# Moving the adaLN gate's pieces, one weight sum and the DRAM sums in a hybrid-head block

## The chip, the cores and the metric

The kernel runs on one core of a Trainium2 chip, as one program. The metric is the device time of one execution in microseconds (us), the median of several runs. PE is TensorE (matmuls), PEld its weight loads, DVE is VectorE, ACT is ScalarE, POOL is GpSimd, SP is SyncE, which only issues DMAs here. ACT and POOL issue DMAs too.

## The reference

One layer with 512 tokens, width 2048, all in float32. `c` is one row of 2048, `w_ada` is 2048 x 12288.

```
mod = silu(c) @ w_ada + b_ada;   sh1, sc1, gt1, sh2, sc2, gt2 = split(mod, 6)
h   = rms_norm(x, g_mix) * (1 + sc1) + sh1
... h @ w_in -> a recurrent group and an attention group -> mix
x   = x + gt1 * (mix @ w_out)
h2  = rms_norm(x, g_ffn) * (1 + sc2) + sh2
gate, up = split(h2 @ w_up, 2)                 # w_up 2048 x 11264
x   = x + gt2 * ((silu(gate) * up) @ w_down)   # w_down 5632 x 2048
```

The change touches how `gt2` is computed and spread, and how the weights of the last two products are summed.

## The kernel before

Every matmul is done in three parts: an operand is split into a high part, rounded to the fast float format by ACT (`hi`, L248), and a rest, taken by DVE (`lo`, L249); PE adds hi*hi, hi*lo and lo*hi. `wsplit` does this for weights; each call leaves its two instructions in `tail_hi` and `tail_lo`, after which other work can be ordered (`tc.issue_after`).

The order of each engine's instructions is made when the program is built, by priority and by which buffers are free; `tc.high_priority(offset=...)` moves a piece of work ahead. A tile that finds no free buffer of its tag waits for the release of an older one. Each engine then runs its list in that order.

The work goes through stages: input projection, heads and recurrence, output projection (`wo`), then two ordinary groups of the up projection (`up0`, `up1`, by `fm_group`, steps 0 to 15 each), then ten upper blocks (`NBLK`), then the down projection in four phases.

*The upper blocks* multiply quarter blocks in Strassen's manner, with seven products in place of eight. In block `b` the products go in the order 4, 5, 1, 7, 6, 2, 3, numbered i = 0 to 6 in the schedule; each has eight steps j, and a hook `(i, j)` is work placed behind step j of the i-th product. Four weight units of 2 MB each (U_A, U_C, U_B, U_D) are loaded by SP into six tiles of 1 MB, two with the tag `raw` and four with `raw2`; `IN_RAW` says which units go to `raw`. DVE adds units to one another (`sum_unit`, L1144, two instructions a sum) before products 5, 7, 6 and 3. Products leave PSUM as pages `us` and `uu` of the tag `c`. This tag has 16 pages, 8 of which hold the second operand through all blocks. Finished blocks are transposed and written to DRAM as `td` (`back`, `keep_act`) in the next block.

*gt2* is a matrix-vector product done on DVE: the class `Gt2` takes 64 pieces of 128 x 512 weights, times the matching quarter of silu(c) (`gt2_r_None`, read from DRAM with broadcast), six or seven in each block (`GT2_N`). Loads are issued by ACT (L192), pieces run on DVE (L200) at the hooks `GT2_STEPS`. At most four pages are live, and each piece asks for the next load. `gt2_sum` adds the partial sums to a 128 x 16 tile. `gt2_spread`, called at the fourth step of the first down phase, writes this tile to DRAM transposed, so that each float lands by itself (L1313, four DMAs of POOL), and reads it back as four broadcast tiles `gt2b` (L1317), which are needed at the end of the third phase.

*DRAM sums.* The down projection is also done in Strassen's manner, and needs sums of its weight quarters. They are made in DRAM, for eleven parts q: `sums24(q, 0)` copies two quarters (SP, L1080 and L1081), `sums24(q, 1)` and `(q, 2)` add a quarter each by accumulating DMAs of POOL (L1073), and `(q, 3)` adds one sum to the other. They hang on the half products of the upper blocks (`SUMS_AT`, `SUMS_PER`).

*The first down phase* computes products 4 and 5 in turn, 22 steps. Product 4's weights come into `raw` (two tiles), product 5's into `raw2`; product 5 needs the sum of both (L1281), which frees product 4's tile for the next load (L1249).

Of the kernel before, what the change touches and what calls it, by code (L numbers as in the profile page):

```python
# [31 lines left out]
SH1, SC1, GT1, SH2, SC2, GT2 = range(6)  # L32
# [24 lines left out]
KEEP = (2, 8, 2)  # L57
GT2_STEPS = ((4, 4), (4, 6), (5, 0), (5, 2), (5, 4), (5, 6), (6, 0))
GT2_N = (6, 6, 6, 6, 6, 6, 7, 7, 7, 7)
SUMS_AT, SUMS_PER = 24, 10  # L60
BU_PART = (0, 5, 10, 16)
# [9 lines left out]
def block_kernel(ctx, tc, xT, crow, adaT, vecs, bfr, w1, wyr, wqkv0, wqkv, wgate, wout, wup0, wups, wdn, outT):  # L71
# [105 lines left out]
    class Gt2:  # L177
        def __init__(self, pieces):
            self.items, self.live, self.pages = [], 0, {}
            for n, (r, i) in enumerate(pieces):  # L180
                if n == 0 or pieces[n - 1][0] != r:
                    self.items.append((r, None))
                self.items.append((r, i))
            self.pieces = list(pieces)

        def loads(self):
            while self.items and self.live < 4:
                r, i = self.items.pop(0)
                cs = slice(r * S, (r + 1) * S)
                t = page(f"gt2_{r}_{i}", "d")  # L190
                with tc.issue_after(tail_hi[-1]):
                    nc.scalar.dma_start(out=t, in_=c_d[:, cs].broadcast_to([P, S]) if i is None else adaT[GT2 * KT + i, :, cs])  # L192
                self.pages[r, i] = t
                self.live += 1

        def piece(self):
            r, i = self.pieces.pop(0)
            t, c = self.pages.pop((r, i)), self.pages[r, None]
            with tc.issue_after(tail_lo[-1]), tc.high_priority(offset=AHEAD):
                nc.vector.scalar_tensor_tensor(out=t, in0=t, scalar=1.0, in1=c, op0=ALU.mult, op1=ALU.mult,  # L200
                                               accum_out=gt2_acc[:, r, i:i + 1])
            self.live -= 2 if not self.pieces or self.pieces[0][0] != r else 1
            self.loads()
# [12 lines left out]

    tail_lo, tail_hi = [], []

    def ada_some(n, ahead=True):
# [35 lines left out]
    def stream(src, kts, width, name, raw_hook=None, ahead=AHEAD):  # L255
        for q in range(len(kts) // 4):
            with tc.high_priority(offset=ahead):
                raw = wp.tile([P, 2048], F32, tag="raw", name=f"{name}r{q}", bufs=RAW)
                nc.sync.dma_start(out=raw[:, :4 * width], in_=src[kts[q * 4] // 4])
            if raw_hook:  # L260
# [814 lines left out]
    def sums24(q, n):  # L1075
        if n == 0:
            with tc.issue_after(up_loads[-1]):
                for i in range(2):
# [18 lines left out]
    for gi in range(STD):  # L1097
        hk = {}
        if gi == 0:
# [3 lines left out]
            add(hk, R1STEP[1], lambda: r1.append(r1_spread()))  # L1103
            add(hk, X_STEPS[3], lambda: x1_by_tokens(3))
        for j in range(4):
            add(hk, T_STEPS[gi][j], lambda j=j + 4 * gi: make_t(j))
# [11 lines left out]
    U_A, U_C, U_B, U_D = range(4)  # L1118
    IN_RAW = (2, 4, 9, 11)
    ORDER = (4, 5, 1, 7, 6, 2, 3)  # L1120
# [4 lines left out]
    def load_unit(b, u):  # L1125
        tiles = []
        mine = len(loads) % 12 in IN_RAW
        loads.append((b, u))
# [17 lines left out]
    def prod_weights(p, b, un):  # L1146
        with tc.high_priority(offset=AHEAD):
# [11 lines left out]
            elif p == 2:  # L1159
                un[U_D] = load_unit(b, U_D)  # L1160
            else:
                sum_unit(un[U_D], un[U_A])
            src = un[{4: U_A, 5: U_A, 1: U_B, 7: U_C, 6: U_A, 2: U_D, 3: U_D}[p]]
        for q in range(4):
# [17 lines left out]
    for b in range(NBLK):  # L1182
        un, keep_ = {}, {}
        gt2 = Gt2(gt2_left[:GT2_N[b]])
        del gt2_left[:GT2_N[b]]
        add(hk, (4, 1), gt2.loads)
        for _, at in zip(range(GT2_N[b]), GT2_STEPS):
            add(hk, at, gt2.piece)
        for i, p in enumerate(ORDER):
# [3 lines left out]
            for j, hi, lo in prod_weights(p, b, un):  # L1193
# [8 lines left out]
                if j % 4 == 3:  # L1202
                    n = halves - SUMS_AT
                    halves += 1
                    if 0 <= n < SUMS_PER * NQ and n % 2 == 0 and n % SUMS_PER < 8:
                        sums24(n // SUMS_PER, n % SUMS_PER // 2)
            if b + i == 0:
# [102 lines left out]
    def gt2_spread():  # L1310
        gd = drp.tile([KT, P], F32, name="gt2d")
        for a in range(4):
            nc.gpsimd.dma_start(out=gd[4 * a:4 * a + 4].rearrange("k p -> p k"), in_=mods[GT2][:, 4 * a:4 * a + 4])  # L1313
        gv = gd.rearrange("(a k) p -> a k p", k=4)
# [150 lines left out]
```

## Time and profile before

| | us |
|---|---|
| median of 3 runs | 2070.2 (2069.98 to 2072.98) |
| the profiled execution | 2063.58, its span 2061.9 |
| PE, DVE, ACT busy | 2017.4, 1676.1, 983.7 |
| upper blocks | 816.8 to 1614.2 |
| first down phase | 1614.2 to 1757.0 |

The profile is one execution, so its stretches add up to the span, not to the median. Times in rows of a chain or a timeline are from the span's start. A row of waits reads: engine and line that waited, what ended the wait, total, number of waits, longest. A name such as `up_2p` leaves out the block's number: the PSUM tile of product 2; `up_3l` is the lo part of the fourth quarter of a product's weights, and `dq_3r` a weight tile of part 3 of the down projection, of any product.

### The profile page before, as it was taken

What the parts mean: (1) busy time and instruction counts of PE and PEld (TensorE: products, weight loads), DVE (VectorE), ACT (ScalarE), POOL (GpSimd) and SP (SyncE); (2) the same over time, 40 slices, a digit from 0 to 9 for tenths busy, and PEclk for the clock granted to TensorE, in tenths of its full rate; (3) what the DMA queues carried; (4) which work ended last, traced back from release to release, by engine and by line L of the source; (5) the groups of instructions that cost most, each with busy time, mean ns of one, the idle gap of its engine ahead of it and who ended that gap; (6) DMA issues with size and microseconds to landing.
All of it is one profiled execution on the core that took longest, in us unless ns stands there. A gap on an engine that the chain in (4) does not pass through costs nothing.

```text
span 2061.9 us, 25612 instructions
## 1 busy us (share of the span) xinstructions
PE 2017.4 (98%) x9329; PEld 1690.5 (82%) x9329; DVE 1676.1 (81%) x2300; ACT 983.7 (48%) x1361; POOL 108.5 (5%) x142
## 2 busy tenths in 40 slices
PE   9999999999999999999999999999999889999998
PEld 7889998888888888887888788878878768888887
DVE  8999768987687779797797797897887857777786
ACT  4433447764522366444444444544444435545443
POOL 0000001111000000001000000010000010000000
PEclk9999999999999999999999999999999999999999
DMA  9989766767588762449989977997985787777793
GB/s 350 355 299 334 247 212 221 231 217 249 191 277 315 267 225 89 136 135 284 252 203 299 267 193 242 259 255 235 251 237 169 193 221 240 260 252 254 266 327 120
DMA packets 173779, 496.33 MB, mean 241 GB/s; under 512 B 18546, under 2 KB 41234, under 8 KB 169555
## 3 DMA queue, kind: packets, MB, share of 16 engines
q1 hardware_dynamic: 151252, 434.80, 62.2%
q0 software_dynamic: 11168, 39.60, 10.9%
q10 hardware_dynamic: 11232, 20.30, 3.2%
q8 instruction: 73, 1.20, 0.2%
q14 instruction: 54, 0.44, 0.1%
HBM read 458.93 MB, written 93.36 MB: 268 GB/s over the span
## 4 chain that ended last, share of the span: by engine, by line
PE 61%; DVE 21%; DMA 8%; issue 8%; ACT 1%; POOL 1%; SPq 0%; ACTq 0%; DVEq 0%; POOLq 0%
PE up_5p L253 5%; PE up_1p L253 5%; PE w1p L253 4%; DVE uw L1144 4%; PE up_7p L253 3%; PE dn6p L253 3%; PE dn3p L253 3%; PE dn2p L253 3%; PE dn1p L253 3%; PE dn7p L253 3%; PE yr1p L253 2%; PE yr0p L253 2%; PE up0p L253 2%; PE wo2p L253 2%; PE wo3p L253 2%
## 5 line engine op out<-in xcount | busy, mean ns | idle before, releaser
L1144 DVE TENSOR_TENSOR uw<-uw,uw 128x2048 f32<-128x2048 f32 x80 | 182.7, 2294 | 0.0
L248 ACT ACTIVATE up_0h<-uw 128x1024 fp32r<-128x1024 f32 x70 | 74.3, 1062 | 157.3 <-DVE uw L1144 65.6
L162 DVE SCALAR_TENSOR_TENSOR ada<-ada,c_b 128x1024 f32<-128x1024 f32 x96 | 116.3, 1222 | 31.0 <-DMA ada<-in_adaT 30.5
L248 ACT ACTIVATE up_1h<-uw 128x1024 fp32r<-128x1024 f32 x70 | 74.2, 1059 | 95.2 <-PE up_5p L253 16.5
L249 DVE TENSOR_TENSOR up_2l<-uw,up_2h 128x1024 fp32r<-128x1024 f32 x70 | 85.9, 1226 | 38.9 <-ACT up_2h L248 38.6
L249 DVE TENSOR_TENSOR up_1l<-uw,up_1h 128x1024 fp32r<-128x1024 f32 x70 | 85.8, 1225 | 32.2 <-ACT up_1h L248 32.2
L248 ACT ACTIVATE up_3h<-uw 128x1024 fp32r<-128x1024 f32 x70 | 74.3, 1061 | 67.5 <-PE up_2p L253 13.9
L248 ACT ACTIVATE up_2h<-uw 128x1024 fp32r<-128x1024 f32 x70 | 74.1, 1059 | 58.0 <-PE up_3p L253 13.2
L249 DVE TENSOR_TENSOR up_0l<-uw,up_0h 128x1024 fp32r<-128x1024 f32 x70 | 85.8, 1225 | 17.8 <-ACT up_0h L248 17.7
L249 DVE TENSOR_TENSOR up_3l<-uw,up_3h 128x1024 fp32r<-128x1024 f32 x70 | 85.7, 1225 | 14.9 <-ACT up_3h L248 14.2
L1073 POOL DMA_DIRECT2D s2d<-in_wdn x44 | 36.4, 833 | 632.3 <-DMA s2d<-in_wdn 632.3
L200 DVE SCALAR_TENSOR_TENSOR gt<-gt,gt_None 128x512 f32<-128x512 f32 x64 | 44.1, 688 | 18.1 <-DMA gt<-in_adaT 12.5
L253 PE MATMUL w1p<-hpl,w1h 128*128 128x512 f32 x128 | 49.8, 389 | 0.0
L253 PE MATMUL w1p<-hph,w1l 128*128 128x512 f32 x128 | 49.8, 389 | 0.0
L172 DVE SCALAR_TENSOR_TENSOR ada<-ada,c_b 128x1024 f32<-128x1024 f32 x32 | 39.1, 1221 | 4.1 <-DMA ada<-in_adaT 4.1
L253 PE MATMUL w1p<-hph,w1h 128*128 128x512 f32 x128 | 42.4, 391 | 0.0
L172 DVE SCALAR_TENSOR_TENSOR adf<-adf,c_b 128x1024 f32<-128x1024 f32 x32 | 39.1, 1222 | 0.4 <-DMA adf<-in_adaT 0.4
L606 ACT ACTIVATE bt<-bt,nm 128x128 f32<-128x128 f32 (+3 forms) x32 | 18.0, 561 | 40.1 <-DVE nm L604 39.8
L685 DVE SCALAR_TENSOR_TENSOR ba<-bw,sh,ba 128x512 f32<-128x512 f32 x45 | 32.8, 750 | 3.3 <-DMA bw<-in_w 2.2
L951 DVE SCALAR_TENSOR_TENSOR bu_acc<-bu,mod,bu_acc 128x512 f32<-128x512 f32 x30 | 22.5, 750 | 13.3 <-DMA bu<-in_wup 12.8
L253 PEld LDWEIGHTS w1p<-hph,w1h 128*128 128x128 f32 x128 | 23.9, 188 | 5.5 <-ACT hph L413 0.7
L413 ACT ACTIVATE hph<-x,A 128x512 fp32r<-128x512 f32 x16 | 11.6, 725 | 35.0 <-DVE A L410 35.0
(2291 smaller groups left out, 6651.5 us busy)
## 6 DMA issues: line engine op xcount, KB each, us to landing
uw<-in_wups SPq DMA_DIRECT2D x160, 512.0 KB, 7.1
ada<-in_adaT SPq DMA_DIRECT2D x128, 512.0 KB, 5.6
s2d<-in_wdn POOLq DMA_DIRECT2D x44, 512.0 KB, 7.9
adf<-in_adaT SPq DMA_DIRECT2D x32, 512.0 KB, 6.3
gt<-in_adaT ACTq DMA_DIRECT2D x64, 256.0 KB, 6.6
s2d<-in_wdn SPq DMA_DIRECT2D x22, 512.0 KB, 10.4
s4d<-in_wdn SPq DMA_DIRECT2D x22, 512.0 KB, 11.1
s4d<-s2d POOLq DMA_DIRECT2D x22, 512.0 KB, 9.4
```

The lines of the kernel that those rows point to most:

```text
L162: nc.vector.scalar_tensor_tensor(out=t, in0=t, scalar=1.0, in1=cs, op0=ALU.mult, op1=ALU.mult, accum_out=ac)
L172: nc.vector.scalar_tensor_tensor(out=t, in0=t, scalar=1.0, in1=c_b[:, cs], op0=ALU.mult, op1=ALU.mult, accum_out=ada_acc[j][:, hf, i:i + 1])
L200: nc.vector.scalar_tensor_tensor(out=t, in0=t, scalar=1.0, in1=c, op0=ALU.mult, op1=ALU.mult, accum_out=gt2_acc[:, r, i:i + 1])
L248: tail_hi.append(nc.scalar.activation(R(hi[:, :n]), raw_ap, AF.Copy).ins)
L249: tail_lo.append(nc.vector.tensor_sub(R(lo[:, :n]), raw_ap, hi[:, :n]).ins)
L253: nc.tensor.matmul(ps, lhsT=R(l), rhs=R(r), start=start, stop=stop)
L413: nc.scalar.activation(R(h), xt, AF.Copy, scale=a)
L606: nc.scalar.activation(p[:, :n], p[:, :n], AF.Exp, scale=-1.0, bias=nm, accum_out=sm)
L685: nc.vector.scalar_tensor_tensor(out=ba[j], in0=src, scalar=s1, in1=ba[j], op0=ALU.mult, op1=ALU.add)
L951: nc.vector.scalar_tensor_tensor(out=a, in0=src, scalar=s2, in1=a, op0=ALU.mult, op1=ALU.add)
L1073: nc.gpsimd.dma_start(out=out[:, cs], in_=src[:, cs], accum_op=ALU.add)
L1144: nc.vector.tensor_add(d_, d_, s_)
```

## The change

- `Gt2`: the loads begin at hook (3, 3) in place of (4, 1); six pages may be live in place of four, the first two of a block taken from the tag `c`; the pieces run at (4, 1), (4, 2), (4, 3), (4, 5), (4, 7), (5, 1), (5, 3).
- The sum for product 3 goes into U_A and product 3 reads U_A; before it went into U_D. With it, the units that use `raw` follow a period of 8, not 12.
- `gt2_spread` writes gt2 to DRAM by one DMA of SP in place of four of POOL.
- The DRAM sums of part 0 are made in the groups `up0` (steps 1, 8, 15) and `up1` (step 6); those of the other ten parts begin at half product 4, one every 13 halves.

```diff
-GT2_STEPS = ((4, 4), (4, 6), (5, 0), (5, 2), (5, 4), (5, 6), (6, 0))
+GT2_STEPS = ((4, 1), (4, 2), (4, 3), (4, 5), (4, 7), (5, 1), (5, 3))
-SUMS_AT, SUMS_PER = 24, 10
+SUMS_AT, SUMS_PER = 4, 13
+SUMS_STEPS = ((1, 8, 15), (6,))
...
-            self.items, self.live, self.pages = [], 0, {}
+            self.items, self.live, self.pages, self.tags = [], 0, {}, ["c", "c"]
...
-            while self.items and self.live < 4:
+            while self.items and self.live < 6:
...
-                t = page(f"gt2_{r}_{i}", "d")
+                t = page(f"gt2_{r}_{i}", self.tags.pop(0) if self.tags else "d")
...
-            self.live -= 2 if not self.pieces or self.pieces[0][0] != r else 1
+            self.live -= 1 if self.pieces and self.pieces[0][0] == r else 2
...
-            with tc.issue_after(up_loads[-1]):
+            with tc.issue_after((up_loads or stream_loads)[-1]):
...
+        for i, n in enumerate(SUMS_STEPS[gi]):
+            add(hk, n, lambda i=i + 3 * gi: sums24(0, i))
...
-    IN_RAW = (2, 4, 9, 11)
+    IN_RAW = (2, 4)
...
-        mine = len(loads) % 12 in IN_RAW
+        mine = len(loads) % 8 in IN_RAW
...
-                sum_unit(un[U_D], un[U_A])
-            src = un[{4: U_A, 5: U_A, 1: U_B, 7: U_C, 6: U_A, 2: U_D, 3: U_D}[p]]
+                sum_unit(un[U_A], un[U_D])
+            src = un[{4: U_A, 5: U_A, 1: U_B, 7: U_C, 6: U_A, 2: U_D, 3: U_A}[p]]
...
-        add(hk, (4, 1), gt2.loads)
+        add(hk, (3, 3), gt2.loads)
...
-                    if 0 <= n < SUMS_PER * NQ and n % 2 == 0 and n % SUMS_PER < 8:
-                        sums24(n // SUMS_PER, n % SUMS_PER // 2)
+                    if 0 <= n < SUMS_PER * (NQ - 1) and n % SUMS_PER % 3 == 0 and n % SUMS_PER < 12:
+                        sums24(1 + n // SUMS_PER, n % SUMS_PER // 3)
...
-        for a in range(4):
-            nc.gpsimd.dma_start(out=gd[4 * a:4 * a + 4].rearrange("k p -> p k"), in_=mods[GT2][:, 4 * a:4 * a + 4])
+        nc.sync.dma_start(out=gd.rearrange("k p -> p k"), in_=mods[GT2])
```

More of the change, by code (lines that the diff above doesn't have):

```diff
@@ L217, in block_kernel @@
     tail_lo, tail_hi = [], []
+    stream_loads = []
     def ada_some(n, ahead=True):
@@ L258, in stream @@
                 raw = wp.tile([P, 2048], F32, tag="raw", name=f"{name}r{q}", bufs=RAW)
-                nc.sync.dma_start(out=raw[:, :4 * width], in_=src[kts[q * 4] // 4])
+                ld = nc.sync.dma_start(out=raw[:, :4 * width], in_=src[kts[q * 4] // 4])
+                stream_loads.append(ld.ins)
             if raw_hook:
```

## The prediction

> **What bounds the kernel now.** I read the page's busy table first, then the time by stretches, then who waited for whom, then the chain that ended last in the two places where PE loses time.
>
> ```profile
> span 2061.9 us, 25612 instructions
> PE 2017.4 (98%) x9329; PEld 1690.5 (82%) x9329; DVE 1676.1 (81%) x2300; ACT 983.7 (48%) x1361; POOL 108.5 (5%) x142
> ```
>
> PE is busy 2017.4 of 2061.9 us. None of the edits touches a matmul, so all that can be won is PE's idle time. The stretches below are cut where PE starts each of the ten upper blocks; the last two rows are the first and the second phase of the down projection. The columns are length, busy time of PE, PEld, DVE, ACT, POOL, granted clock, DMA share and GB/s.
>
> ```profile
> core 0: us, PE busy (x) PEld busy (x) DVE busy (x) ACT busy (x) POOL busy (x), PEclk, DMA share, GB/s
> 816.80:893.00 76.20, 76.20 (x338) 63.09 (x337) 64.80 (x73) 36.62 (x41) 0.00 (x0) 1.00 0.46 146
> 893.00:973.60 80.60, 78.96 (x353) 64.32 (x352) 67.03 (x74) 37.72 (x44) 4.58 (x6) 1.00 0.67 190
> 973.60:1052.70 79.10, 78.64 (x354) 64.60 (x352) 68.01 (x76) 37.72 (x44) 5.53 (x7) 1.00 0.86 249
> 1052.70:1131.20 78.50, 78.37 (x354) 64.61 (x353) 67.78 (x76) 37.97 (x44) 9.84 (x12) 1.00 0.99 262
> 1131.20:1210.80 79.60, 79.05 (x354) 64.44 (x353) 67.43 (x76) 37.85 (x44) 4.91 (x6) 1.00 0.86 246
> 1210.80:1289.30 78.50, 78.37 (x354) 64.61 (x353) 67.75 (x77) 37.95 (x44) 4.94 (x6) 1.00 0.81 224
> 1289.30:1371.20 81.90, 78.89 (x353) 64.42 (x352) 67.79 (x76) 37.70 (x44) 9.85 (x12) 1.00 0.99 257
> 1371.20:1450.40 79.20, 78.56 (x354) 64.59 (x354) 68.19 (x78) 38.11 (x44) 4.92 (x6) 1.00 0.85 249
> 1450.40:1532.80 82.40, 79.06 (x354) 64.44 (x352) 68.30 (x78) 37.86 (x44) 9.82 (x12) 1.00 0.99 256
> 1532.80:1614.20 81.40, 79.28 (x354) 64.44 (x352) 68.10 (x78) 38.71 (x46) 0.00 (x0) 1.00 0.56 181
> 1614.20:1757.00 142.80, 128.39 (x545) 101.25 (x544) 98.71 (x96) 63.30 (x79) 10.57 (x16) 0.96 0.79 217
> 1757.00:1876.70 119.70, 119.70 (x529) 99.06 (x528) 90.49 (x78) 59.30 (x72) 0.00 (x0) 1.00 0.72 245
> ```
>
> A block without stalls takes 78.5 us (two of them do). The nine blocks behind the first exceed it by 2.1 + 0.6 + 0 + 1.1 + 0 + 3.4 + 0.7 + 3.9 + 2.9 = 14.7 us. The two down phases have the same 22 steps. The second runs without a gap in 119.7 us; the first takes 142.8, of which 1.8 are the last block's 16 transposes (an estimate, from the 0.11 us between their starts), so it loses 21.3 us. These two sums, 36 us, are the stake.
>
> ```profile
> PE up_2p L253 <- DVE up_3l L249: 4.2, 3, 1.7
> PE up_3p L253 <- DVE up_1l L249: 3.5, 4, 1.2
> ...
> DVE gt L200 <- DMA gt<-in_adaT: 12.5, 11, 2.1
> ...
> ACT up_0h L248 <- DVE uw L1144: 65.6, 17, 5.7
> ...
> 1330.37 8.28 DMA gt<-in_adaT
> ...
> 1341.15 10.94 DMA gt<-in_adaT
> ...
> 1352.88 2.20 DVE uw L1144
> ...
> 827.85 10.88 PE up_5p L253 x48
> ```
>
> In the blocks, PE waits in products 2 and 3 for DVE's lo splits. DVE runs in order, and a gt2 piece (L200) that stands before a split waits for its load: 12.5 us in 11 waits. The chain of the dear block at 1289 to 1371 goes through two such loads, then the sum of U_D (L1144), which stands between splits of products 2 and 3. A product is 10.88 us, a step 1.36.
>
> ```profile
> PE dn4p L253 <- ACT dq_3w0h L248: 8.3, 1, 8.3
> ...
> 1643.96 0.61 PE L253 MATMUL dn5p<-dq_1w1h,dq_1tl 128*128 128x512 f32 x2
> ...
> 1625.39 4.36 DMA dq_2r<-in_wdn
> ...
> 1637.20 16.54 DMA dq_3r<-in_wdn
> ...
> 1659.37 9.45 DMA dq_4r<-in_wdn
> ...
> 1674.45 8.62 DMA dq_5r<-in_wdn
> ...
> 1688.71 6.49 DMA dq_6r<-in_wdn
> ...
> L1313 POOL DMA_DIRECT2D gt2d<-mod x4: 757/766/852, 1626.5 to 1665.4; - x4
> DMA to landing us min/median/max: 11.1/13.0/13.5
> ```
>
> In the first down phase the chain is load after load: product 4's next weight tile has only two buffers and can be fetched only once the sum for product 5 has read the old one. Such a load takes 4.36 us where nothing disturbs it. The four behind it take 12.2, 5.1, 4.3 and 2.1 us more, 23.7 in all, which covers the 21.3 lost. They are slow exactly while the four writes of gt2 to DRAM are under way (L1313, first 1626.5, last 1665.4 plus 13). What the DMA engines moved in the stretches between the reading of such a write and its landing, and in the undisturbed rest of the phase:
>
> ```profile
> 1631.00:1639.00 8.00, 7.75 (x34) 5.94 (x33) 7.13 (x8) 3.59 (x4) 1.23 (x2) 1.00 1.11 87
> ...
> 1648.00:1654.00 6.00, 1.10 (x2) 0.50 (x2) 1.12 (x1) 1.21 (x2) 0.00 (x0) 0.54 0.90 124
> 1658.00:1666.00 8.00, 8.00 (x35) 6.54 (x35) 4.02 (x4) 2.64 (x3) 0.61 (x1) 0.96 0.63 78
> ...
> 1672.00:1679.00 7.00, 5.34 (x23) 3.79 (x22) 4.41 (x3) 2.00 (x2) 0.65 (x2) 1.00 0.90 94
> 1708.00:1757.00 49.00, 49.00 (x217) 40.56 (x217) 38.29 (x34) 26.10 (x34) 0.00 (x0) 1.00 0.73 247
> ```
>
> 8 KB in single floats holds up all queues for 8 + 6 + 8 + 7 = 29 us, at 78 to 124 GB/s against the 247 that the phase takes when it runs freely. The 8.3 us wait also drops the granted clock to 0.54 behind it.
>
> **The change, part by part.**
>
> *gt2 pieces and their pages.* The same 64 pieces, six or seven a block, and the same loads. Before, the shared row of c and three pieces are asked for at step (4,1), and the first piece comes three steps, 4.1 us, later; each further load waits on ACT for a page that a piece frees, and its piece follows six steps, 8.2 us, behind. After, the row and five pieces go out at (3,3), six steps ahead of the first piece at (4,1); the sixth and seventh are asked for at (4,1) and (4,2) and used eight and nine steps, 10.9 and 12.2 us, later.
>
> ```profile
> DMA to landing us min/median/max: 2.9/6.6/12.4
> ```
>
> That row is the landing time of the gt loads. The median is covered everywhere; only the slowest (blocks where the DRAM copies of s2d and s4d go out just then) will still make DVE wait a little. ACT holds one or two late loads a block instead of three or four, so its hi splits behind them are freer. A price on the other side: 1.5 MB now leave at (3,3) beside the next block's weights, and the first two pages come from the pool that U2's tile needs at the end of product 6; that tile then waits for the last piece, at (5,1) or (5,3). DVE reaches these positions about when product 6 ends, so I cost it at nothing, at most 1 us in blocks of seven pieces.
>
> *The sum for product 3 goes into U_A.* Same two DVE instructions of 2.2 us. Into U_D each half had to wait until product 2's splits had read it; into U_A it needs only product 6's splits done and U_D landed, both earlier. So the sum leaves the narrow place between product 2 and product 3. U_D is free before U_A now, the order is swapped, and the buffer choice (period 8 instead of 12) fits that; loads have a product or more of lead, cost nothing.
>
> *DRAM sums.* Same bytes, one of eleven sums moved into the two groups ahead of the blocks, the others every 13 halves instead of 10. The DMA share of the first block is 0.46 and of others up to 0.99, so the work goes where there is room; the SP queue ahead of the blocks carries 2 MB more among stream loads. I cost it at nothing; if its cover there is gone, one weight load of 4.36 us comes late once.
>
> Of the blocks' 14.7 us, 12.3 lie in the four with over 2 us each, all of this kind. Bounds: 13 gained; 3 lost if the earlier burst only moves the waits. What is late next is DVE itself, 68 of 78.5 us busy. I take 8 gained, nearer the upper end, because the two waits are removed where the chain has them.
>
> *gt2 to DRAM by SP.* Four POOL instructions of 0.77 us go, one SP instruction comes. POOL no longer holds the last td writes. On SP the write stands among the weight loads. Its input is ready before POOL's first write at 1626.5, and SP's next load goes out later:
>
> ```profile
> 1629.06 0.80 SPq L1249 DMA_DIRECT2D dq_4r<-in_wdn  x2
> ```
>
> So SP waits for nothing new; but in its queue the loads now stand behind 2048 single floats. No row shows such a write from SP. Bounds: as short as one of the four (8 us), or as long as all (29 us). With a start at 1627.5 and 3 us for what queued up, the one load exposed, issued at 1637.2, lands at 1659.5 in the long case: it takes 22.3 us, 17.9 too long, 5.8 less than the 23.7 of before. In the short case it is undisturbed, and nearly all 21.3 are won. Twice the 29 is rival 4 below. I take the middle, 18.5 us: lands at 1649, 7.4 too long, 16.3 less than before; scaled by 21.3/23.7 about 14 us won. Reason: the elements are the same, but the set-up and the final receipt of each of the four (a landing of 13 us against 6 to 8 us of slow traffic) are paid once.
>
> **Sum.** -8 - 14 = -22 us. The profiled execution took 2063.6 us (span 2061.9 and 1.7 around it); the median of the runs shown, 2070.2, is 6.6 above it, and I take the difference over unchanged: 2070.2 - 22 = 2048.
>
> **The rivals.**
> 1. *The price of the write is kept.* Nothing is saved but the repeats: -5.8 there, -8 in the blocks, 2056. For it: the packets of all queues stand still together, as if one place took the floats one by one. The Trainium skill says the same: by "DMA: Bandwidth & Descriptors", Rules for kernel authors, a strided last dimension makes one descriptor for each element, and by its section "Issuing engines are not separate DMA queues" another issuing engine saves only issue time. The stretches above, slow for all queues at once, agree with the second.
> 2. *The write from SP is nearly free.* -20 there, -10 in the blocks: 2040. For it: a 512-float write took 13 us, far more than its bytes; against: no row of SP with single floats.
> 3. *The burst at (3,3) collides.* Blocks gain 0 to 1, the write 14: 2056. For it: landings up to 12.4 us; against: 4 us more lead.
> 4. *Slower: each float costs twice as much from SP,* since each goes as a packet of its own and SP's own loads stand behind it. 58 us from 1627.5, plus 3: the load takes 51 us, 47 too long, 23 more than before; with -8 that is +15, 2085. It decides from a blockade of 43 us on, where the load is 32 us late: 1.5 times the 29 seen.
> 5. *Nothing happens:* the stalls reappear behind DVE, the write costs 35 us; 2066 to 2074.
>
> **How the numbers follow.** Forecast 0.42, rivals 0.17, 0.13, 0.08, 0.12, 0.08. 0.2% (4 us) is about what a measurement of this kernel can tell from no change. Faster: 0.42 + 0.16 + 0.13 + 0.07 = 0.78; slower: 0.12; the same: 0.10. Range 2038 to 2074: from rival 2 up to rival 5; rival 4 and a tip of rival 2 stay out. The forecast's own range is 2042 to 2054.
>
> **What would show it.** Blocks of 78.5 to 79.5 us, DVE's waits for gt under 5 us, no PE wait in product 3: the first two edits right. One gt2d row from SP with a landing near 20 us, one slow dq load, first down phase near 128 us: the write right. A landing over 45 us, or a PE wait over 25 us at the fourth step, would make the forecast wrong; so would blocks that stay at 81 us, with ACT or DVE waiting at product 6.

## The result, and the profile after

The changed kernel takes 2061.6 us (median of 5 runs, 2059.2 to 2064.6) against 2070.0 (2067.7 to 2073.0) for the kernel before on the same chip: a ratio of 0.996, 95% interval 0.9945 to 0.9974. It is faster by 8.4 us, where 22 were forecast; the time lies inside the range given.

The page of the changed kernel: PE has the same work, and its span is only 2.2 us shorter than that of before. The profiled execution of before (2063.6) lay under all five runs of this comparison, so the two profiles show 2.2 of the 8.4 us. They serve to say where time came and went; how much the change is worth is read from the medians.

```profile
span 2059.7 us, 25583 instructions
PE 2017.1 (98%) x9329; PEld 1695.0 (82%) x9329; DVE 1674.8 (81%) x2300; ACT 987.2 (48%) x1361; POOL 107.0 (5%) x138
```

The stretches of the changed kernel, cut where PE starts an upper block, with the columns of the prediction's table (length, busy PE, PEld, DVE, ACT, POOL, granted clock, DMA share, GB/s). The last row is the first down phase.

```profile
828.75:904.91 76.16, 76.16 (x337) 63.08 (x336) 66.57 (x75) 36.64 (x41) 4.11 (x5) 1.00 0.73 204
...
983.08:1061.23 78.15, 78.15 (x353) 64.59 (x352) 67.47 (x76) 38.30 (x44) 4.95 (x6) 1.00 0.80 225
...
1139.38:1219.22 79.84, 78.92 (x354) 64.35 (x352) 67.38 (x75) 38.07 (x44) 9.07 (x11) 1.00 0.94 251
1219.22:1303.24 84.02, 79.80 (x353) 65.52 (x352) 67.81 (x76) 38.20 (x44) 4.95 (x6) 0.98 0.74 218
1303.24:1381.44 78.20, 78.20 (x353) 64.50 (x352) 68.07 (x77) 38.41 (x44) 4.92 (x6) 1.00 0.74 217
1381.44:1466.73 85.29, 81.24 (x353) 65.97 (x352) 68.39 (x78) 38.20 (x44) 4.94 (x6) 0.96 0.74 221
1466.73:1546.52 79.79, 78.72 (x353) 64.43 (x352) 68.05 (x77) 38.10 (x44) 4.92 (x6) 1.00 0.81 225
...
1626.20:1755.26 129.06, 124.00 (x546) 101.67 (x545) 98.09 (x92) 65.64 (x82) 7.46 (x12) 0.99 0.75 255
```

Three things happened. The first block starts at 828.75 instead of 816.80: 12.0 us lost ahead of the blocks, a place to which the prediction gave no stall. The first down phase became 13.6 us shorter, as forecast. The ten blocks together did not change (797.5 us, before 797.6; the same blocks took 800.5 in another execution, e2 below, so 3 us are within what executions differ by). Four blocks reach 78.15 to 78.2 us, below the 78.5 that I had taken for a block without stalls, but blocks 5 and 7 (counted from 0) cost 84.0 and 85.3.

*Ahead of the blocks.* The waits of PE and of DVE in this place (engine, line and what ended the wait, total, times, longest), then SP's queue, then the chain (start, length):

```profile
PE up0p L255 <- ACT hrh L908: 8.0, 1, 8.0
```

```profile
DVE ada L163 <- DMA ada<-in_adaT: 15.7, 4, 12.7
```

```profile
705.02 0.63 SPq L1083 DMA_DIRECT2D s2d<-in_wdn  x1
705.70 0.73 SPq L1084 DMA_DIRECT2D s4d<-in_wdn  x1
706.47 0.73 SPq L1083 DMA_DIRECT2D s2d<-in_wdn  x1
707.25 0.61 SPq L1084 DMA_DIRECT2D s4d<-in_wdn  x1
...
711.05 1.47 SPq L152 DMA_DIRECT2D ada<-in_adaT  x2
```

```profile
703.51 5.38 DMA ada<-in_adaT
...
712.19 17.88 DMA ada<-in_adaT
...
733.07 0.73 ACT hrh L908
...
733.84 14.41 PE up0p L255 x48
```

The same place in the chain of the kernel before:

```profile
725.43 10.88 PE up0p L253 x48
```

The four copies of part 0 stand right ahead of the last two loads of `w_ada`. The load ahead of them took 5.38 us, the last 17.88. DVE needs it for the second norm's scale, from which `hr` is made, and PE can't begin `up0` without `hr`. Before, PE had no wait there. PE begins `up0` 8.4 us later than before, and its first 48 matmuls take 14.41 us in place of 10.88: the granted clock is 0.77 from 733.8 to 748.3. The wait and the slow clock behind it make the 12.0 us.

*In blocks 5 and 7.* All waits of PE in the ten blocks, and DVE's for gt2's pieces:

```profile
PE up_2p L255 <- DVE up_0l L251: 4.2, 1, 4.2
PE up_2p L255 <- DVE up_1l L251: 4.1, 1, 4.1
PE up_6p L255 <- DVE up_2l L251: 2.6, 3, 1.1
```

```profile
DVE gt L201 <- DMA gt<-in_adaT: 15.9, 11, 5.0
```

The waits of product 3 are gone, as forecast; two large ones in product 2 are new. The chain of block 5, SP's queue just before it, and ACT's reads of the shared row of silu(c) at that time (two, one for each of two 512-rows of gt2):

```profile
1265.49 10.55 DMA gt<-in_adaT
...
1276.13 0.09 DVE gt L201
...
1276.83 1.31 DVE uw L1149
...
1278.95 1.23 DVE up_0l L251
...
1280.22 12.30 PE up_2p L255 x47
```

```profile
1262.94 0.53 SPq L1084 DMA_DIRECT2D s4d<-in_wdn  x1
1263.51 0.60 SPq L1083 DMA_DIRECT2D s2d<-in_wdn  x1
1264.15 0.60 SPq L1084 DMA_DIRECT2D s4d<-in_wdn  x1
```

```profile
L193 ACTq DMA_DIRECT2D gt_None<-c_d x2: 332/534/736, 1251.8 to 1255.1; - x2
```

A gt load asked for at 1265.49, just after three DRAM copies had gone out and as POOL's first accumulation began (1265.6), lands 10.55 us later; DVE waits 5.0 us for it. The piece that needs it stands in DVE's list ahead of half a sum and of product 2's split.

*The write.* The instruction on SP and its landing, then the late load in the chain, then PE's wait for it:

```profile
L1317 SPq DMA_DIRECT2D gt2d<-mod x1: 382/382/382, 1614.2 to 1614.2; - x1
...
DMA to landing us min/median/max: 12.3/12.3/12.3
```

```profile
1615.96 13.04 DMA dq_0r<-in_wdn
```

```profile
PE dn4p L255 <- ACT dq_0w0h L250: 4.0, 1, 4.0
```

One late load remains of the four. The write itself left 12 us ahead of the phase, during product 3 of the last block.

### The profile page after: what moved, and what is told of

It reads as the page before. It is cut to its first block, busy times and chain, and to the rows that moved or that the text cites. A ratio compares the mean times of both kernels' runs of the same rounds, so it can differ in the third digit from the quotient of the medians.

```text
span 2059.7 us, 25583 instructions
## 1 busy us (share of the span) xinstructions
PE 2017.1 (98%) x9329; PEld 1695.0 (82%) x9329; DVE 1674.8 (81%) x2300; ACT 987.2 (48%) x1361; POOL 107.0 (5%) x138
## 3 DMA queue, kind: packets, MB, share of 16 engines
q1 hardware_dynamic: 153316, 434.80, 61.6%
q0 software_dynamic: 11040, 39.59, 10.8%
## 4 chain that ended last, share of the span: by engine, by line
PE 72%; DVE 9%; DMA 9%; issue 8%; ACT 1%; POOL 1%; SPq 0%; DVEq 0%; POOLq 0%; ACTq 0%
PE up_2p L255 5%; PE up_5p L255 5%; PE up_4p L255 5%; PE up_3p L255 5%; PE w1p L255 4%; PE up_1p L255 4%; PE up_7p L255 4%; DMA ada<-in_adaT 4%; PE up_6p L255 3%; PE dn6p L255 3%; PE dn3p L255 3%; PE dn1p L255 3%; PE dn2p L255 3%; PE dn7p L255 3%; PE dn5p L255 3%
## 5 line engine op out<-in xcount | busy, mean ns | idle before, releaser
L251 DVE TENSOR_TENSOR up_1l<-uw,up_1h 128x1024 fp32r<-128x1024 f32 x70 | 85.3, 1219 | 30.3 <-ACT up_1h L250 30.3
L251 DVE TENSOR_TENSOR up_2l<-uw,up_2h 128x1024 fp32r<-128x1024 f32 x70 | 85.3, 1219 | 22.7 <-ACT up_2h L250 22.7
L251 DVE TENSOR_TENSOR up_3l<-uw,up_3h 128x1024 fp32r<-128x1024 f32 x70 | 85.3, 1218 | 14.7 <-ACT up_3h L250 14.7
L954 DVE SCALAR_TENSOR_TENSOR bu_acc<-bu,mod,bu_acc 128x512 f32<-128x512 f32 x30 | 22.5, 748 | 13.5 <-DMA bu<-in_wup 13.0
L255 PEld LDWEIGHTS w1p<-hpl,w1h 128*128 128x128 f32 x128 | 24.0, 188 | 5.0
## 6 DMA issues: line engine op xcount, KB each, us to landing
s2d<-in_wdn SPq DMA_DIRECT2D x22, 512.0 KB, 10.5
```

The source lines that it names most:

```text
L251: tail_lo.append(nc.vector.tensor_sub(R(lo[:, :n]), raw_ap, hi[:, :n]).ins)
L255: nc.tensor.matmul(ps, lhsT=R(l), rhs=R(r), start=start, stop=stop)
L954: nc.vector.scalar_tensor_tensor(out=a, in0=src, scalar=s2, in1=a, op0=ALU.mult, op1=ALU.add)
```

## The experiments

All ratios are to the kernel before on the same chip, with 95% intervals. The stretches are from each one's profile, in us, cut where PE starts the first block, ends product 3 of the last, and starts product 1 of the down projection.

| kernel | ratio | first block starts | ten blocks | first down phase | rest |
|---|---|---|---|---|---|
| before | 1 | 816.8 | 797.6 | 142.7 | 304.9 |
| changed | 0.9960 (0.9945 to 0.9974) | 828.8 | 797.5 | 129.1 | 304.4 |
| e1 part 0 late | 0.9924 (0.9907 to 0.9941) | 817.4 | 796.9 | 127.6 | 304.5 |
| e2 write alone | 0.9940 (0.9923 to 0.9957) | 818.4 | 800.5 | 130.7 | 304.4 |
| e3 pieces alone | 0.9979 (0.9967 to 0.9992) | 819.6 | 801.7 | 134.6 | 304.5 |
| e4 sums alone | 1.0055 (1.0038 to 1.0072) | 830.8 | 801.1 | 141.0 | 304.6 |
| e5 cadence 14 | 0.9906 (0.9889 to 0.9924) | 815.0 | 790.2 | 127.6 | 304.5 |
| e6 rows | 0.9915 (0.9900 to 0.9930) | 817.8 | 798.0 | 128.0 | 304.5 |
| e7 four by SP | 0.9921 (0.9906 to 0.9937) | 818.1 | 793.8 | 127.8 | 304.2 |
| e8 unit undone | 0.9919 (0.9905 to 0.9933) | 816.4 | 800.1 | 125.7 | 304.5 |
| e9 write later in the text | 0.9922 (0.9900 to 0.9943) | 816.6 | 796.9 | 128.5 | 304.5 |
| e10 e9, cadence 14 | 0.9884 (0.9863 to 0.9905) | 817.2 | 789.8 | 128.6 | 304.5 |
| e11 write held | 0.9923 (0.9905 to 0.9941) | 819.9 | 796.2 | 121.3 | 312.4 |
| e12 e11, cadence 14 | 0.9905 (0.9886 to 0.9924) | 829.7 | 790.5 | 121.3 | 313.9 |

**e1: part 0's copies later.**

```diff
-SUMS_STEPS = ((1, 8, 15), (6,))
+SUMS_STEPS = ((), (1, 6, 11, 15))
...
-            add(hk, n, lambda i=i + 3 * gi: sums24(0, i))
+            add(hk, n, lambda i=i: sums24(0, i))
```

> The changed kernel with one edit: the DRAM sums of part 0 hang on steps 1, 6, 11 and 15 of the second group ahead of the blocks (up1) instead of steps 1, 8, 15 of the first (up0) and 6 of up1. Theory T1 (place of the copies): in the changed kernel the four copies of part 0 went out at 705 to 708 us, right ahead of the last ada loads of that stage, which then landed 17 to 18 us after their issue; DVE waited 12.65 us for one of them and PE stood still 8.0 us at up0p, so that the first block began at 828.75 instead of 816.80. With the copies some 20 us later no load of the stage that is waited for stands behind them: the first block begins at 817 to 819 us, PE has no wait over 1 us between 725 and 775, and the time is about 2061.6 - 11 = 2050 (2047 to 2053). Rival R1 (amount, not place): 2 MB more in these two groups cost 12 us wherever they stand; the wait comes back at up1 or at the first block, the first block begins after 826, and the time is 2059 to 2064. Rival R2: the 12 us are won at the start and the first blocks lose part of it, since part 0's accumulations now lie on the last step before them: 2053 to 2058.

Measured 2051.2 us against 2066.7. PE waits nowhere between 700 and 817.4, the first block starts at 817.4, and the first copy leaves at

```profile
752.27 0.64 SPq L1083 DMA_DIRECT2D s2d<-in_wdn  x1
```

T1 holds: the same 2 MB, 47 us later, cost nothing at the start. From the first matmul of the output projection to the first block PE takes 275.3 us in the kernel before, 286.9 in the changed one and 275.3 again in e1, so 11.6 us are won back. A tip of R2 is seen: the first block takes 78.5 instead of 76.2 us. By the ratios e1 gains 0.36% on the changed kernel, 7.5 us, with some 0.2% of uncertainty; the 11 expected are at its edge, and R2's price lies inside.

e1 moves part 0's copies and the accumulations that follow them together, so it doesn't say which of the two made the load late. In the changed kernel the slowest copies took 11.1 us and had landed by about 718.4; POOL's accumulations went out at 714.1 and 717.3; the load was under way from 712.2 to 730.1.

**e4: the DRAM sums alone** (the kernel before with the diff's `SUMS_AT`, `SUMS_PER`, `SUMS_STEPS` and the hooks that use them).

> The kernel before with one group of edits: the DRAM sums of part 0 in the two groups ahead of the blocks, the others every 13 halves from half 4 on. Theory T1: the copies of part 0 cost about 12 us ahead of the first block (it begins at 827 to 830 us instead of 816.8; PE waits 6 to 9 us at up0p; last ada loads land 15 us or more after issue), and the spread wins 2 to 6 us in the blocks, where fewer copies meet gt loads: 2070 + 12 - 4 = 2078 (2075 to 2082), slower. Rival R1: the late ada loads need another edit of the change as well (none touches that stage, so I see no way), or were chance: the first block begins at 817 to 819 and the time is 2064 to 2069. Rival R2: the spread costs in the blocks as well, since the sums now meet gt2's loads at (4,1) in more blocks: 2082 to 2088.

Measured 2079.2 against 2066.7: this edit alone is 0.55% slower. Its one wait of PE ahead of the blocks:

```profile
PE up0p L255 <- ACT hrh L908: 9.4, 1, 9.4
```

The start, 830.8, is just above T1's 827 to 830: PE takes 287.9 us from the output projection to the first block, 12.6 more than before. The 2 to 6 us that T1 gave to the blocks are not won (801.1). With e1, both undoing it and doing it alone show the 12 us.

**e3: the pieces alone** (the kernel before with the diff's `GT2_STEPS`, `Gt2` and the hook (3, 3)).

> The kernel before with one group of edits: gt2's loads start at (3,3), up to six pages live (two of tag c), pieces at the new steps; the DRAM sums stay every 10 halves from half 24 on, the sum for product 3 stays in U_D, the write stays four by POOL. Theory T1: the pieces' new steps take DVE's waits for gt away only where no DRAM copy goes out between the sixth load's issue and its landing. The changed kernel had two such collisions (PE waits of 4.2 and 4.1 us in product 2, blocks of 84.0 and 85.3 us beside 78.2 elsewhere); with the old cadence of the copies the collisions fall into other blocks. I expect the nine blocks behind the first to lose 8 to 14 us over their 78.2 to 78.5 each instead of 14.7, and the time at 2063 to 2070; new PE waits of 3 us or more in product 2, each behind an SP copy issued within 5 us of the late gt load. Rival R1: the early pieces help by themselves, and the two stalls came from the new cadence of the sums alone: no PE wait over 2 us in product 2, the blocks lose under 6 us, 2059 to 2062. Rival R2: the pieces at the new steps are the cause of the stalls whatever the copies do (the page pool, the sixth and seventh load): blocks lose more than before, 2070 to 2076.

Measured 2062.9 against 2066.7. The blocks win nothing (801.7, e2's unchanged ones 800.5), but not as any theory said: no wait over 1.5 us in product 2, and small waits in product 7 of six blocks instead. What was won lies in the first down phase, 8.1 us, which I had not expected: gt2 is done earlier, and POOL's four writes begin at 1619.5 instead of 1626.5, against a phase that begins 7 us later. That this earlier start shortens the phase is read from these times; no run tests it apart. PE's waits in the blocks, and the writes:

```profile
PE up_7p L253 <- DVE up_3l L249: 3.8, 6, 0.8
PE up_2p L253 <- DVE up_2l L249: 2.9, 3, 1.5
PE up_7p L253 <- DVE up_2l L249: 2.7, 4, 0.8
```

```profile
L1313 POOL DMA_DIRECT2D gt2d<-mod x4: 750/773/836, 1619.5 to 1651.1; - x4
```

**e5 and e6: what makes the two dear blocks.** e5 moves the copies, e6 moves the passage from one 512-row of gt2 to the next out of block 5; both start from e1.

```diff
-SUMS_AT, SUMS_PER = 4, 13
+SUMS_AT, SUMS_PER = 2, 14          # e5
...
-GT2_N = (6, 6, 6, 6, 6, 6, 7, 7, 7, 7)
+GT2_N = (7, 7, 6, 6, 6, 6, 6, 6, 7, 7)   # e6
```

> The kernel of e1 (part 0's sums late) with one edit: the other DRAM sums come every 14 halves from half 2 on instead of every 13 from half 4, so that their four copies leave at the same place of each block, 63 to 75 us after the block's start. In e1 two blocks took 83.9 and 83.4 us instead of 78.2, each with a PE wait of 3 to 4 us in product 2; in both the copies left at 39 to 46 us, just as the last gt loads were asked for, and both are blocks in which gt2's pieces pass from one 512-row to the next. Theory T1 (it takes both: a row change asks for two loads more late, and copies at that time stretch them): with the copies elsewhere both waits go and no block is over 80 us; the ten blocks take about 797 - 10 = 787 us and the ratio to the kernel before is 0.9924 - 0.005 = 0.987 to 0.988. Rival R1 (the row change alone makes the wait): two blocks of 82 to 85 us stay, ratio 0.991 to 0.994. Rival R2: the regular place costs elsewhere (last part ends later, its accumulations meet the first loads of the down phase): the blocks win 8 to 10, the first down phase loses 4 to 10, ratio 0.989 to 0.993.

> The kernel of e1 with one edit: seven gt2 pieces in blocks 0, 1, 8 and 9 and six in blocks 2 to 7 (before: seven in the last four). The passage from one 512-row of gt2 to the next now falls on the border between two blocks at row 2, so that only blocks 2 and 7 hold one instead of 2, 5 and 7. The copies stay where they were. Theory T1 (row change and copies together): block 5, with copies but no row change, falls from 83.9 to 78.2 to 80 us and its PE wait of 3.9 us in product 2 goes; block 7 (row change and copies) keeps 82 to 86 us; ratio to the kernel before about 0.9924 - 0.0025 = 0.990. Rival R1 (copies at that place are enough): block 5 stays at 82 to 85 us, ratio 0.992 to 0.994. Rival R2 (the seventh piece makes it): block 5 unchanged, and blocks 0 and 1 gain waits of their own; ratio 0.993 or more.

By stretches, of e5 the first block and blocks 5 and 7, of e6 blocks 5 and 7; then PE's wait in e6's block 7:

```profile
814.96:899.08 84.12, 78.94 (x338) 64.03 (x337) 74.84 (x86) 40.40 (x49) 1.66 (x2) 0.98 0.57 175
...
1211.73:1289.89 78.16, 78.16 (x354) 64.58 (x352) 67.48 (x76) 38.23 (x44) 4.97 (x6) 1.00 0.79 228
...
1368.04:1446.15 78.11, 78.11 (x354) 64.57 (x352) 68.13 (x78) 38.30 (x44) 4.94 (x6) 1.00 0.82 228
```

```profile
1212.80:1291.12 78.32, 78.32 (x354) 64.50 (x352) 67.40 (x75) 38.42 (x44) 4.13 (x5) 1.00 0.72 219
...
1369.26:1455.87 86.61, 81.21 (x354) 66.28 (x352) 67.84 (x76) 38.08 (x44) 4.93 (x6) 0.96 0.74 216
```

```profile
PE up_2p L255 <- DVE up_0l L251: 5.4, 1, 5.4
```

It takes both. Block 5 with the copies but without the row change: 78.3 us. Blocks 5 and 7 with the row change but without the copies: 78.1 to 78.2. Block 7 with both: 86.6. ("The copies" means a part's copies with the accumulations behind them; they always moved together.)

The times of the late load in block 5 show why. Without copies near (e5) it lands 3.5 us after it is asked for. With them (e6, no row change) it takes 8.4 us and DVE wants it 9.3 us after, so it is covered. With both (changed kernel) it takes 10.55 us and DVE wants it 5.7 us after. A row change holds two pages of the six for shared rows of c. So in a block of six pieces already the fifth piece's load has to wait for a page: it is asked for at (4,1) and used at (4,7), six steps later, where otherwise only the sixth piece's is late and has eight. That two loads are late is not enough: block 6, with seven pieces, no row change and copies in the same place, asks for two loads late too; DVE uses the first of them 9.5 us after, no load there takes longer than 9.2, and the block takes 78.2 us. In block 7 of the changed kernel the slack is 9.0 us, and the load takes 12.96.

Here T1 was right in both. Its price for e5 was missed: the first block pays 84.1 us, so that 790.2 was reached and not 787. The chain of that block goes through a write `td<-sg` of 12.70 us, in a stretch where the accumulations of parts 0 and 1 follow one another closely (as read from their issue times; not tested apart). In e1, e7, e8, e9 and e11 this write takes 6.6 to 7.6 us and the first block 77.5 to 78.5; in e6 9.1 and 80.8. By the medians e5 is 0.2% below e1, with intervals that overlap.

**e2: the write alone.**

```diff
-        for a in range(4):
-            nc.gpsimd.dma_start(out=gd[4 * a:4 * a + 4].rearrange("k p -> p k"), in_=mods[GT2][:, 4 * a:4 * a + 4])
+        nc.sync.dma_start(out=gd.rearrange("k p -> p k"), in_=mods[GT2])
```

> The kernel before with one edit: gt2 goes to DRAM in one write by SP instead of four by POOL. Theory T1: this write alone carries the 13.6 us that the first down phase became shorter (142.8 to 129.2 us); the blocks and all ahead of them stay as before, so about 2070.0 - 13.5 = 2056.5 (2054 to 2059), with a landing of the gt2d row of 12 to 20 us. Rival R1: in the changed kernel the write was issued during product 3 of the last block, at 1614, only because gt2's pieces end earlier there (last step (5,1) or (5,3) instead of (6,0)); with the old steps it goes out later, its blockade falls on the loads of the first steps of the down phase, and only 4 to 8 us are won: 2062 to 2066. Rival R2: the single floats from SP cost as much as from POOL and the phase gained from the other edits (POOL free of late td writes, DVE): within 3 us of 2070.

Measured 2055.3 against 2066.7, 11.4 us; the first down phase is 12.0 us shorter. T1 holds. The write falls into the phase itself here, at 1630.8, and lands 17.0 us later. One load is still late, dq_3r (11.2 us), and PE waits for it:

```profile
PE dn4p L253 <- ACT dq_3w0h L248: 4.6, 1, 4.6
```

**e7: four writes by SP** (e1 with the loop over `a` of before, on `nc.sync`).

> The kernel of e1 with one edit: gt2 goes to DRAM in four writes of 512 floats as in the kernel before, but all from SP, instead of one write of 2048 floats. It parts the two reasons why the write became cheap (first down phase 127.6 us in e1, 142.7 in the kernel before, where four writes from POOL went out one behind another at 1626.5, 1640.3, 1654.0 and 1665.4, each landing 11 to 13.5 us later). Theory T1 (the price is one per write, 12 us whether 512 or 2048 floats, and POOL sent them one after another): from SP the four leave within 3 us of each other and overlap; if they share the time, the last lands within 12 to 18 us of the first, the down phase takes 127 to 130 us and the time is that of e1. Rival R1 (one price per write that can't overlap): the last lands 45 to 52 us behind the first, the first down phase takes 135 to 143 us and 8 to 15 us are lost against e1. Rival R2 (it was the earlier start of the write in e1, at 1602, not its engine or number): as T1 in time, with a landing of each of 12 us at about the same start.

SP's queue at the writes, and their landings:

```profile
1599.85 2.04 SPq L1318 DMA_DIRECT2D gt2d<-mod  x4
```

```profile
DMA to landing us min/median/max: 10.5/10.9/11.0
```

The four leave within 2 us and land 10.5 to 11.0 us after their issue, together; the phase takes 127.8 us. So it was not the smaller number of writes that made the price fall; the four are cheap when they are under way together. POOL's four stood 11 to 14 us apart, each behind the landing of the one before. R2, the earlier start, would give the same times and is not excluded by e7; for one write it is by e2, which starts as late as POOL's first and still wins 12.0 us. Why POOL sends each write only behind the landing of the one before, no run shows.

**e8: the unit undone** (e1 with `sum_unit(un[U_D], un[U_A])`, product 3 from U_D and the period of 12).

> The kernel of e1 with one part of the change undone: the sum for product 3 goes into U_D again, and the choice of buffers has period 12 again. Theory T1 (the sum of U_D stands between the splits of products 2 and 3 and has to wait for product 2's splits to be read; with gt2's early pieces alone this left PE waits in product 7 and product 2 of almost every block, blocks of 80 to 82 us): the nine blocks behind the first grow from an average of 79.8 to 81 us, 8 to 14 us in all, mostly as PE waits of 0.5 to 1 us in products 2, 3 and 7; ratio to the kernel before 0.996 to 0.999. Rival R1 (the unit changes nothing once the pieces are early): within 3 us of e1, ratio 0.991 to 0.994. Rival R2 (it is worth the two large waits only): blocks 5 and 7 change, all others stay at 78.2 to 79.8.

Measured 2048.7 against 2065.5, the ratio of e1: R1. In its profile the blocks take 3.2 us more than in e1 (blocks 4, 5 and 7 take 82.9 to 83.6) and the first down phase 1.9 less; e1, e7, e9 and e11, with the same blocks, differ by 3.1 us, so this is no clear loss.

**e9 and e11: the write where loads have more lead.** e9 calls `gt2_spread` at the third step of product 6 instead of the first phase; e11 also holds the write behind the loads of that step.

```diff
-                if (ph, q) == (0, 2):
+                if (ph, q) == (2, 2):                   # e9 and e11
...
+        with tc.issue_after(dn_loads[-1]):              # e11
+            nc.sync.dma_start(out=gd.rearrange("k p -> p k"), in_=mods[GT2])
```

> The kernel of e1 with one edit: the one write of gt2 by SP and the four reads behind it are emitted at the third step of the third down phase (product 6) instead of the third step of the first. In e1 the write went out at 1602.25 and landed 11.95 us later; dq_0r, issued 1.8 us behind it, took 12.7 us, and PE waited 3.7 us for it, with a slower clock in the steps behind. Theory T1 (what the write costs still is that one late load; product 6 has no second product in its steps, so its loads go out further ahead and 12 us are covered): the first down phase falls from 127.6 us to 122 to 124, the rest stays at 304.5 to 306, and the ratio to the kernel before falls from 0.9924 to about 0.990. Rival R1 (dq_0r is late anyway: its buffer comes free late at the end of the last block): the phase stays at 126 to 128 and nothing is won, ratio 0.991 to 0.994. Rival R2 (product 6 has no cover either): the 4 to 6 us move there, rest 309 to 311, ratio 0.991 to 0.994.

e9 says nothing on its question: the write still left at 1601.5 and it is e1 once more. Its blocks 5 and 7 (81.6 and 85.0 us, e1 83.9 and 83.4) show how far such stalls vary between executions.

> The kernel of e1 with one edit: the one write of gt2 by SP is held on SP behind the loads of the third step of the third down phase. In e9, where only its place in the program was moved there, the write still went out at 1601.5, because the order of SP's queue is set by what is ready first, so e9 didn't test this. Theory T1 (what the write still costs is the one late load: PE waited 3.7 us for dq_0r, issued 1.8 us behind the write and landed 12.7 us later; product 6's loads have the lead to cover 12 us): the write goes out after 1860, dq_0r lands within 8 us of its issue, the first down phase takes 122 to 125 us instead of 127.6, the rest 304 to 306, and the ratio to the kernel before is about 0.9905. Rival R1 (dq_0r is late anyway): the phase stays at 126 to 129, ratio 0.991 to 0.994. Rival R2 (no cover in product 6 either): the phase falls, the rest grows by 3 to 10 us, ratio 0.991 to 0.995.

The first down phase of e11, and PE's wait in product 6:

```profile
1616.16:1737.49 121.33, 121.33 (x545) 100.68 (x544) 95.40 (x90) 63.00 (x79) 5.30 (x8) 1.00 0.71 243
```

```profile
PE dn6p L255 <- ACT dq_1w0h L250: 6.2, 1, 6.2
```

Without the write the first phase runs without a gap in 121.3 us, so the write costs 6.3 us there in e1 (127.6). In product 6 it costs 7.9 (rest 312.4 against 304.5): R2. My ground for T1, that product 6's loads have the lead, was wrong.

**e10 and e12: the versions with both.** e10 is e9 with `SUMS_AT, SUMS_PER = 4, 14`, e12 is e11 with `3, 14`.

> The kernel of e1 with two edits: the DRAM sums every 14 halves from half 4 on (e5 had 14 from half 2), and the write of gt2 at the third step of the third down phase (as in e9). In e5 the eight blocks behind the first took 78.1 to 78.2 us each but the first 84.1, since the accumulations of parts 0 and 1 fell together there, and the last 81.0. Theory T1: with part 1 two halves later the first block takes 76 to 79 us, the others 78.2, the last 79 to 81; ten blocks in 782 to 786 us; with the later write the first down phase in 122 to 124: together about 14 to 16 us below e1 in the profile, ratio to the kernel before 0.985 to 0.987. Rival R1 (half 4 brings the copies back beside the late gt loads in some block): a block of 82 us or more with a PE wait in product 2, ratio 0.988 to 0.990. Rival R2 (part 10 now ends with the last half; its accumulations meet the first loads of the down phase): down phase 128 us or more, ratio 0.988 to 0.991.

> The kernel of e1 with both edits: the DRAM sums every 14 halves from half 3 on (from half 2 in e5: first block 84.1 us, the others 78.2; from half 4 in e10: first block 77.5, the others 78.2 to 79.4), and the write held as in e11. Theory T1: ten blocks in 784 to 790 us as in e5 and e10 (790.2 and 789.8) or a little less, the first down phase in 122 to 125, rest 304 to 306: 10 to 14 us below e1 in the profile, ratio to the kernel before 0.985 to 0.988. Rival R1: half 3 gives the first block's collision of e5 and nothing else is won: 0.988 to 0.990. Rival R2: the held write costs in the third phase: rest over 308 us, ratio 0.988 to 0.992.

By its median e10 is the fastest kernel run, 2042.2 us against 2066.6; its interval overlaps those of e5 and e12. Since e9's edit moves nothing, this is part 0 late and the cadence of 14 alone: blocks in 789.8, as e5, with 77.5 for the first. The last takes 82.5, and the first down phase stays at 128.6. In e12 the held write takes away what the cadence gives (rest 313.9). Its profile is of the slowest of its six executions (2057.1, median 2047.8) and begins the blocks 12.3 us later than e1's. Of these, 5.4 lie ahead of the output projection, where nothing was edited. Behind it the chain goes through the same write `td<-sg` as in e5, here 16.36 us, to a wait of 3.7 us in `up1` and of 3.2 in the first block (82.5 us). Whether half 3 makes that write late was not tested.

## Why the prediction was right in direction and wrong in size

*DRAM sums: "I cost it at nothing; if its cover there is gone, one weight load of 4.36 us comes late once."* This step failed, and it is most of the miss: 12.0 us lost, shown by e1 and e4 (11.6 and 12.6 by the time from the output projection to the first block). I priced the 2 MB by the DMA share of the blocks, where there was room, and by one late weight load in the place that they came to. What is loaded beside them there are the last pieces of `w_ada`. The last one took 17.9 us, where the six loads in this place took at most 5.6 before, and its reader leads to the scale without which `up0` can't begin. PE waited 8.0 us and lost the rest to a slower clock. That part 0's sums in that place make the load late is shown; whether by the copies or by the accumulations is open. The profile before shows no wait of PE there, but it does show how thin the cover was. In DVE's timeline of the kernel before the last `ada` piece, the scale `a`, and the next instruction (ACT makes the first part of `hr` with the scale at 723.2):

```profile
718.58 1.23 DVE L162 SCALAR_TENSOR_TENSOR ada<-ada,c_b 128x1024 f32<-128x1024 f32 x1
...
721.29 0.17 DVE L899 SCALAR_TENSOR_TENSOR a<-mod,vec 128x16 f32<-128x16 f32 x1
723.43 0.75 DVE L989 SCALAR_TENSOR_TENSOR x<-wo3p,mod,rstd_att 128x512 f32<-128x512 f32 x1 [1.97 <-PE wo3p L253]
```

That is 1.7 us of slack between the scale, ready at 721.5, and its first use, for a load that took some 12 us longer.

*Blocks: -8 taken, bounds 13 won to 3 lost.* Measured 0 in the profiles, with 3 us of spread. This is the second term that failed. Its mechanism was half right: PE's waits in product 3 went, and a block now runs in 78.15 us. The term was mis-sized at "only the slowest (...) will still make DVE wait a little": in two blocks DVE waited 5.0 and 4.1 us. Rival 3's collision did occur, but not from the burst at (3,3): from the late loads of blocks with a row change, beside copies (e5, e6). I had counted the sixth and seventh loads as used eight and nine steps after they were asked for. That holds in blocks without a row change; I had not counted the page of the second shared row, which in block 5 leaves the fifth piece's load six.

*The stall's full price.* Block 7 waited 4.1 us in product 2 and was 7.1 longer than 78.2. The rest is in the clock: 0.96 granted over the block, 0.50 and 0.70 in the two stretches of 4 us from 1444, and PE busy 81.24 us for the work of 78.15. In block 5 a wait of 4.2 us cost 1.7 more, ahead of `up0` one of 8.0 us cost 3.5 more. The prediction had priced waits at their length.

*The write: -14 taken* (the working gives 14.6). Measured -13.6, and -12.0 alone in e2. The forecast put the write into the phase; that case is e2, where its late load took 11.2 us, 6.8 too long, against 7.4 forecast. In the changed kernel the write left before the phase and delayed another load, 13.04 - 4.36 = 8.7 too long. The size was right, though as the middle of two wide bounds (18.5 us between 8 and 29) it was so partly by luck. The reason was right only in part: I gave the price to the set-up and receipt of each of four writes. e7 shows that four cost no more than one when they go out together. Rival 1 fell. By the Trainium skill ("DMA: Bandwidth & Descriptors", Issuing engines are not separate DMA queues) another issuing engine saves only the time of issue, which is usually small next to the DMA itself. Here what the other engine saved was not small: POOL's second write went out 13.8 us after its first, SP's 0.5 us after, though POOL's instruction itself took only 0.77 us.

*The sum for product 3 and the units.* The prediction gave the units no cost and the sum no price of its own; with the pieces it was to bring the 8 us. By the medians it brings nothing beside the early pieces (e8, the same ratio as e1). The waits in product 3 had gone with the pieces already: e3, with the sum still in U_D, has none.

*The parts together.* Alone the write gives -0.60%, the pieces -0.21%, the sums +0.55%, the unit about 0: -0.26%, with the change at -0.40% and each number uncertain by 0.15. The write and the pieces both shorten the first down phase (12.0 and 8.1 us alone, 13.6 together), so there they don't add up in full; that the change is nonetheless slightly better than the sum of its parts lies within the uncertainty.

*The account of the miss.* In the profiles 2.2 us were won where 22 were forecast: 12.0 lost ahead of the blocks and 8 not won in them make the difference. By the medians 8.4 were won. The two differ because the profiled execution of before lay 6.4 us under its median (2063.6 against 2070.0), while that of the changed kernel is its median; the forecast had carried such a difference over unchanged.

What stays open: whether copies or accumulations stretch the loads beside them, and why the last block takes 81 to 82.5 us under a cadence of 14 (part 10's last accumulations lie in its first 20 to 25 us there).

## What to carry to other kernels

Price a moved transfer by the loads that are due beside and behind it where it arrives, and by who waits for them, not by the free bandwidth there: the same 2 MB cost 12 us at one place of SP's queue and, 47 us later, nothing ahead of the blocks and 2.4 us in the first of them. Two things that each fit in a load's slack may not fit together: here copies that stretch it and a row change that shortens its lead; list the blocks in which they meet. Moving a call in the program's text need not move its instruction: read the issue time before a run is taken as an answer.

## What the runs showed of the hardware that I had not expected

A write of 2048 single floats from SP landed in 12.3 us (11.4 to 17.0 over ten runs), as long as one of 512 from POOL (11.1 to 13.5 us), and four of 512 from SP overlapped in 10.5 to 11.0. Counted in packets the order is the other way round: with e2's edit alone the packets of POOL's queue fall by 128 (11168 to 11040) and those of SP's rise by 2064 (151252 to 153316), yet the phase is 12.0 us shorter. The loads issued just behind such a write took 11 to 13 us instead of 4.4 (dq_0r in the changed kernel and in e1, dq_3r in e2). PE waits of 4 us lowered the granted clock behind them enough to cost 1.7 to 3.1 us more, while blocks with waits of up to 1.7 us show 1.00.
